# A hybrid decoder layer: the scaling of the exponentials, the sum of three attention branches and the order of their units are changed

## The chip, the cores and the metric

The kernel runs on one core of a Trainium2 chip as a single launch. The metric is the device time of one execution in microseconds; the median of several runs is given. A profile is one further execution, recorded by the hardware profiler. PE is the matrix engine (PEld its weight loads), DVE the vector engine, ACT the scalar engine, POOL the GpSimd engine, and SP the queue that issues most DMAs. Each engine works through its own instructions in order.

## The reference

One layer for 2048 tokens of width 1024, in float32:

```
h = RMSNorm(x); P = h @ W_in             # columns for three head groups
A: sliding-window attention (window 128, 4 heads, sinks, QK-norm, relative bias)
B: S5 state-space model, GELU, GLU
C: block attention, 4 heads, one key/value head, per block of 128 queries:
   o_cmp = softmax(q k_cmp + bias) v_cmp          # keys compressed 32 -> 1, stride 16
   top 16 of 32 key blocks by the compressed probabilities
   o_sel = softmax(q k_sel + bias) v_sel          # the selected blocks
   o_win = softmax(q k_win + bias) v_win          # the last 512 keys
   o     = gate0 * o_cmp + gate1 * o_sel + gate2 * o_win
x = x + W_out @ concat(RMSNorm(o_A), RMSNorm(o_B), RMSNorm(o_C))
x = x + W_down @ relu(W_up @ RMSNorm(x))^2
```

The compressed keys and values come from a two-layer network over 32 tokens: a hidden layer of 128 with GELU, then 64 outputs.

## The kernel before

The program runs in stages. The front (`phase_front`) computes the projection; in its second half the products of each chunk are merged with the steps of the state-space model (`ssm_steps`). Then a middle stage runs three lists of steps merged evenly with one another: sliding-window attention (`swa_steps`), the GLU (`glu_steps`) and a list with the bias tables and the compression of keys and values (`bias_steps`, `compress_steps`). Then comes block attention with the output projection (`phase_mix`), then the up projection and the down projection, both as seven-product schemes over halves.

Where exactness is wanted, a float32 operand is split into a rounded high part and a low part (fp32r), and a product is the sum of two or three products of parts (`mm3`, lines 76 to 78).

Block attention goes over 16 blocks of 128 queries. For each block the kernel loads and normalises queries and keys (`prep`), computes the compressed branch (`cmp_steps`), from block 8 on selects key blocks (`select`), and then runs four *units*: two pairs of heads of the window branch (up to 640 keys), and two pairs of the selected branch (all keys so far, up to 2048, with a mask in the lower rows of the query operand). A unit has two lists of steps:

- `logits` (lines 860 to 884): for up to 512 keys at a time, two products into one of two PSUM banks (`pq`, lines 875 and 876), one DVE pass that adds the bias, writes the negated logits to a slab in SBUF and keeps the running minimum (line 878), and after the last piece one ACT exponential over the whole slab with its sum (line 883).
- `pv` (lines 886 to 906): for two blocks of 128 keys and two heads, four PE transposes of the exponentials into one PSUM bank (`pp`, line 896, two banks), an ACT copy to the high part (line 899), a DVE subtraction to the low part (line 900), and the value products from both parts (line 904) into a PSUM sum (`po`). These products are given a lower priority (`LAG`).

At the end of each of the three branches, `combine` (lines 908 to 924) copies the sum from PSUM (ACT, line 913), turns it back by four transposes (line 917), multiplies it by gate over sum of exponentials (DVE, line 919), and POOL adds the two parts, high and low of the values, to the block's output (lines 921 and 924).

The order of the work: lists of steps are merged evenly (`merge`). In the loop over blocks, the value products of unit u are merged with the logits of unit u+1, with the steps of the next block that come ahead of its units (`front`: `prep`, the compressed branch, `select`), and with a share of a queue of *finish* steps of older blocks (`finish_steps`: load, scaling, the turn of the mixed row, 48 products with the output weights, the residual sum, the square for the norm). The finish products are fillers: they have a lowered priority. The framework's scheduler takes this order and the priorities, and fixes each engine's order of instructions and the semaphores. For the last block the selected units come first and the window units last.

Buffers of block attention: four slabs of 2048 floats for the exponentials of both branches, PSUM with two banks for logits, two for transposed exponentials, two for sums, one for turns (`pt`) and one for the filler (`pw`). From block 2 on (`open_late`) the output weights are loaded and the norms of the other two head groups are prepared, by steps on DVE (lines 44 to 54).

## Time and profile before

| what | value |
|---|---|
| median of 3 runs | 2577.39 us (2571.8 to 2578.93) |
| the profiled execution | 2574.28 us, its span 2572.5 us |
| busy share of the span | PE 96%, PEld 81%, DVE 69%, ACT 52%, POOL 44% |
| mean granted PE clock | 0.987 |
| front with state-space model | about 0 to 416 us |
| sliding-window attention, GLU, compression | about 416 to 616 us |
| block attention, with the rest of the GLU and the output projection | about 616 to 1277 us |
| up projection | about 1277 to 1955 us |
| down projection | about 1955 to 2572 us |

How to read it: the busy time of an engine counts every instruction from start to end. A product's record is longer than the time until the next one can start, since products are pipelined, so a busy PE is not a PE at its pace. A line in the groups gives the line of the kernel, engine, operation, what is written and read, shape and count; then busy time and mean duration of one; then the idle time of the engine in front of them with what ended it. The chain of waits is the work that ended last, followed back from the end; a piece's time there is counted from the end of the piece before.

### The profile page before, as it was taken

How to read it: one execution, taken by the hardware profiler on the slowest of the kernel's cores; microseconds unless marked ns; L12 is line 12 of the kernel's file. 1: busy time of each engine (PE TensorE's matmuls, PEld its weight loads, DVE VectorE, ACT ScalarE, POOL GpSimd, SP SyncE). 2: the span in 40 equal slices, each digit the busy share in tenths (PEclk: the TensorE clock that was granted, in tenths of full speed). 3: DMA queues.
4: the chain of work that ended last, by engine and by line, in shares of the span. 5: the costliest groups of instructions: out<-in, count | busy, mean ns of one | idle time of the engine just before them, and what ended most of it. 6: DMA issues, size and time to landing. Idle time of an engine off the chain costs nothing.

```text
span 2572.5 us, 38493 instructions
## 1 busy us (share of the span) xinstructions
PE 2475.1 (96%) x12904; PEld 2080.1 (81%) x12904; DVE 1769.6 (69%) x3455; ACT 1324.9 (52%) x2767; POOL 1119.3 (44%) x1168
## 2 busy tenths in 40 slices
PE   8999998999999999999999999899999999999999
PEld 8989997777787777777777888688887888888887
DVE  4744876864787677777465565765557888888886
ACT  5334546765676565655465554544444444344442
POOL 3045222222223233332476767565545344454447
PEclk9999999999989999999999999999999999999999
DMA  6153426221212121221566667755547534444435
GB/s 199 61 126 102 116 89 172 86 60 50 65 64 71 36 67 48 87 66 56 177 204 187 187 185 207 233 163 144 153 130 251 167 93 136 132 132 130 123 98 197
DMA packets 397144, 324.66 MB, mean 126 GB/s; under 512 B 51943, under 2 KB 363885, under 8 KB 395121
## 3 DMA queue, kind: packets, MB, share of 16 engines
q1 hardware_dynamic: 360848, 297.03, 38.6%
q10 hardware_dynamic: 36096, 25.17, 3.1%
q8 instruction: 102, 1.67, 0.3%
q14 instruction: 98, 0.79, 0.1%
HBM read 209.66 MB, written 112.45 MB: 125 GB/s over the span
## 4 chain that ended last, share of the span: by engine, by line
PE 67%; DVE 5%; issue 2%; ACT 2%; DMA 2%; POOL 1%; SPq 0%; DVEq 0%; POOLq 0%; ACTq 0%
PE pdc L1738 7%; PE pdb L1738 7%; PE pda L1738 7%; PE pub L1556 6%; PE puc L1556 6%; PE pua L1556 6%; PE pdd L1738 3%; PE pud L1556 3%; PE pw L76 2%; PE pps L896 2%; PE pos L904 2%; PE pw L77 2%; PE pw L78 2%; DVE sls L878 1%; PE gpm L76 1%
## 5 line engine op out<-in xcount | busy, mean ns | idle before, releaser
L1414 ACT CAST v<-vr 128x512 fp32r<-128x512 f32 x224 | 139.4, 624 | 304.2 <-DMA vr<-vd 148.4
L1415 DVE TENSOR_TENSOR v<-vr,v 128x512 fp32r<-128x512 f32 x224 | 233.1, 1048 | 81.2 <-ACT v L1414 79.2
L1738 PE MATMUL pdc<-dw,v 128*128 128x512 f32 x768 | 187.0, 392 | 4.3 <-ACT dw L1414 3.2
L1738 PE MATMUL pdb<-dw,v 128*128 128x512 f32 x768 | 185.2, 390 | 0.0
L1738 PE MATMUL pda<-dw,v 128*128 128x512 f32 x768 | 184.5, 389 | 0.0
L1527 POOL TENSOR_TENSOR fs<-ur,ur 128x512 f32<-128x512 f32 x64 | 94.8, 1481 | 189.2 <-DMA ur<-in_w_up 152.0
L1738 PEld LDWEIGHTS pdc<-dw,v 128*128 128x128 f32 x768 | 145.3, 189 | 35.4 <-ACT dw L1414 3.7
L1738 PEld LDWEIGHTS pdb<-dw,v 128*128 128x128 f32 x768 | 144.8, 189 | 30.3
L1738 PEld LDWEIGHTS pda<-dw,v 128*128 128x128 f32 x768 | 144.1, 188 | 30.0
L1414 ACT CAST uh<-fs 128x512 fp32r<-128x512 f32 x128 | 78.5, 621 | 152.0 <-PE pub L1556 62.7
L1415 DVE TENSOR_TENSOR ul<-fs,uh 128x512 fp32r<-128x512 f32 x128 | 134.3, 1051 | 22.6 <-ACT uh L1414 22.3
L1415 DVE TENSOR_TENSOR ul<-ur,uh 128x512 fp32r<-128x512 f32 x96 | 101.0, 1053 | 52.3 <-ACT uh L1414 48.5
L900 DVE TENSOR_TENSOR tls<-pps,ths 128x512 fp32r<-128x512 f32 (+1 forms) x144 | 93.2, 658 | 46.0 <-ACT ths L899 37.7
L899 ACT CAST ths<-pps 128x512 fp32r<-128x512 f32 (+1 forms) x144 | 79.5, 565 | 83.4 <-PE pos L904 40.3
L76 PE MATMUL pw<-wo_h,mh 128*128 128x512 f32 x256 | 109.2, 427 | 6.2 <-ACT mh L1251 4.2
L1572 POOL TENSOR_TENSOR ev<-e,e 128x512 f32<-128x512 f32 x64 | 95.9, 1498 | 31.9 <-ACT e L1569 21.9
L1556 PE MATMUL pua<-fh,ul 128*128 128x512 f32 x256 | 100.9, 394 | 5.7 <-DVE ul L1415 5.7
L78 PE MATMUL pw<-wo_h,ml 128*128 128x512 f32 x256 | 105.4, 412 | 0.0
L77 PE MATMUL pw<-wo_l,mh 128*128 128x512 f32 x256 | 105.1, 410 | 0.0
L1556 PE MATMUL puc<-fh,uh 128*128 128x512 f32 x256 | 102.1, 399 | 1.9 <-DVE eu L1565 1.9
L1556 PE MATMUL pub<-fh,uh 128*128 128x512 f32 x256 | 102.1, 399 | 1.6 <-ACT fh L1414 1.6
L1556 PE MATMUL pua<-fh,uh 128*128 128x512 f32 x256 | 101.0, 395 | 2.5 <-ACT e L1576 2.5
(573 smaller groups left out, 7875.3 us busy)
## 6 DMA issues: line engine op xcount, KB each, us to landing
vr<-vd SPq DMA_DIRECT2D x224, 256.0 KB
ur<-in_w_up SPq DMA_DIRECT2D x128, 256.0 KB
vd<-ev SPq DMA_DIRECT2D x128, 256.0 KB
vd<-e ACTq DMA_DIRECT2D x64, 256.0 KB
dr<-in_w_down SPq DMA_DIRECT2D x32, 512.0 KB
x<-in_x SPq DMA_DIRECT2D x16, 512.0 KB
mx<-in_x SPq DMA_DIRECT2D x16, 512.0 KB
x<-mx ACTq DMA_DIRECT2D x16, 512.0 KB
```

Of the source, the lines that this page charges most:

```text
L76: nc.tensor.matmul(out, sh, mh, start=first, stop=False)
L77: nc.tensor.matmul(out, sh, ml, start=False, stop=False)
L78: nc.tensor.matmul(out, sl, mh, start=False, stop=last)
L896: nc.tensor.transpose(pt[:, j, hh], sls[hh][:, (b0 + j) * P:(b0 + j + 1) * P], C["ident"])
L899: nc.scalar.copy(th[:, 0:nb], pt[:, 0:nb])
L900: nc.vector.tensor_tensor(tl[:, 0:nb], pt[:, 0:nb], th[:, 0:nb], op=ALU.subtract)
L1414: nc.scalar.copy(dh, src)
L1415: nc.vector.tensor_tensor(dl, src, dh, op=ALU.subtract)
L1527: nc.gpsimd.tensor_tensor(t, x, y, op=op)
L1556: nc.tensor.matmul(bank[b], w[:, k], h[o][:, k], start=first and k == 0 and n == 0, stop=k == HALF - 1 and n == 2, skip_group_check=True)
L1572: nc.gpsimd.tensor_tensor(tile_("v" + o), x, y, op=op)
L1738: nc.tensor.matmul(bank[b, q], x[:, q, j], y[:, j], start=first and j == 0 and n == 0, stop=j == 1 and n == 2, skip_group_check=True)
```

## The change

In block attention:

- Window and selected branch: after the exponential, DVE takes the reciprocal of each head's sum, and POOL multiplies the whole slab by it and by the gate. The compressed branch is scaled likewise after its reciprocals (`recip`). `combine` is called once for each block, without weights; a DVE reduction adds high and low parts.
- All three branches add into one PSUM sum of the block (`po` moves to `front`); only its first product starts the bank, and the other products of that kind are issued behind it. The bank is released by the copy in `combine`. There is one such bank in place of two; the transposed exponentials have three in place of two.
- The value products of a unit are merged with the logits of the unit two places on. The value products of the compressed branch lie with those of the block's first unit. The window branch has four slabs of its own of 640 floats.
- The turn of an older row (`next_turned`) is placed behind the fifth filler product; the output step writes its squares to SBUF and not to PSUM; the norms in `open_late` are computed by POOL.

In the front and in the middle stage:

- The last four half products of the front come behind the last steps of the state-space model.
- The compression's activations are stored so that a product of the hidden layer reads neighbouring elements; before, it read every eighth one.
- Six empty steps are appended to the list with bias tables and compression, so that its steps come earlier in the merge.

The core of the diff:

```diff
-        run(merge(rest, ssm_steps(tc, C, S, u_st, dkp, dca, tp, ps_g, ps_t)))
+        run(merge(rest[:-4], ssm_steps(tc, C, S, u_st, dkp, dca, tp, ps_g, ps_t)) + rest[-4:])
...
-        X = box["X"] = tp.tile([P, 1040], F32, tag="X", name=f"cX{st}")
-        nc.sync.dma_start(X[:, 1024:1040], cmp_pos[0, st].rearrange("(jj two) d -> (two d) jj", two=2))
+        X = box["X"] = tp.tile([P, 8, 130], F32, tag="X", name=f"cX{st}")
+        for b in range(2):
+            nc.sync.dma_start(X[:, :, 128 + b], cmp_pos[0, st, 16 * b:16 * b + 16].rearrange("(jj two) d -> (two d) jj", two=2))
...
-        nc.scalar.copy(box["X"][:, 512 * q:512 * q + 512], pt.rearrange("p a b -> p (a b)"))
+        nc.scalar.copy(box["X"][:, :, 64 * q:64 * q + 64], pt.rearrange("p a (m j) -> p j (a m)", j=8))
...
-            nc.tensor.matmul(ph, w1[:, jj], X[:, jj:jj + 8 * P + 1:8], start=jj == 0, stop=jj == 15)
+            nc.tensor.matmul(ph, w1[:, jj], X[:, jj % 8, jj // 8:jj // 8 + P + 1], start=jj == 0, stop=jj == 15)
...
                 nc.scalar.activation(x, x, AF.Exp, bias=nm[:, h:h + 1], scale=-1.0, accum_out=den[:, h:h + 1])
+                if gate is not None:
+                    nc.vector.reciprocal(den[:, h:h + 1], den[:, h:h + 1])
+                    nc.gpsimd.tensor_scalar(x, x, den[:, h:h + 1], gate, op0=ALU.mult, op1=ALU.mult)
...
-            pt = self.ps_p.tile([P, 2, 2, P], F32, tag="pp", name=f"pp{name}{b0}", bufs=2)
+            pt = self.ps_p.tile([P, 2, 2, P], F32, tag="pp", name=f"pp{name}{b0}", bufs=3 if self.lag else 2)
...
-                        nc.tensor.matmul(po, v_of(b0 + j), t[:, j].rearrange("p h q -> p (h q)"),
-                                         start=b0 + j == 0 and n == 0, stop=b0 + j == nblk - 1 and n == 1)
+                        opening = b0 + j == 0 and n == 0 and first is not None
+                        begun = first.get("mm") if opening else None
+                        with self.tc.issue_after(begun) if begun is not None else nullcontext():
+                            mm = nc.tensor.matmul(po, v_of(b0 + j), t[:, j].rearrange("p h q -> p (h q)"), start=opening and begun is None,
+                                                  stop=last and b0 + j == nblk - 1 and n == 1, skip_group_check=True)
+                        if opening and begun is None:
+                            first["mm"] = mm.ins
...
+        if w is None:
+            nc.vector.tensor_reduce(acc, pt.rearrange("p h a d -> p h d a"), axis=AX.X, op=ALU.add)
+            return
...
-            rsqrt_into(nc, sm, ra, ss_a, 1.0 / 256, NT, "ra")
-            rsqrt_into(nc, sm, rc, ss_b, 0.25 / 512, NT, "ra")
+            rsqrt_into(nc, sm, ra, ss_a, 1.0 / 256, NT, "ra", nc.gpsimd)
+            rsqrt_into(nc, sm, rc, ss_b, 0.25 / 512, NT, "ra", nc.gpsimd)
...
+                if i >= 8:
+                    pn = box["pn"] = lp.tile([P, 4, P], F32, tag="qd", name=f"pn{i}", bufs=1)
+                    nc.gpsimd.tensor_tensor(pn[:, :, 0:n], slc[:, :, 0:n], den.unsqueeze(2).broadcast_to([P, 4, n]), op=ALU.mult)
+                nc.gpsimd.tensor_tensor(slc[:, :, 0:n], slc[:, :, 0:n], w.unsqueeze(2).broadcast_to([P, 4, n]), op=ALU.mult)
...
-                    box[h] = lp.tile([P, L], F32, tag="sl", name=f"sl{nm_}{i}{h}", bufs=4)
+                    width, tag = (5 * P, "slw") if nm_ == "w" else (L, "sl")
+                    box[h] = lp.tile([P, width], F32, tag=tag, name=f"sl{nm_}{i}{h}", bufs=4)
...
-                nc.scalar.activation(pw, xt, AF.Square, accum_out=box["ss"][:, n:n + 1])
+                nc.scalar.activation(late["fp"].tile([P, 512], F32, tag="sq", name=f"xsq{i}{n}"), xt, AF.Square, accum_out=box["ss"][:, n:n + 1])
...
+            before = late.pop("turn", [])
+            res[8:8] = before
...
-            res[1:1] = late.pop("turn", [])
...
+            res = units(i, *box["q"], box["oc"], box["po_of"])
+            res[0] = (res[0][0], box["cmp"][1] + res[0][1])
...
-            for u in range(3):
-                acc += cuts[u]
-                na, nt = len(ahead) * acc // tot, len(tail) * acc // (tot + len(cur[3][1]))
-                for st in merge(cur[u][1], cur[u + 1][0], ahead[done_a:na], tail[done_t:nt]):
-                    st()
+            for u in range(4):
+                if u == 2 and i + 1 < NT:
+                    ocs[i + 1] = box["oc"]
+                    nxt = units_of(i + 1, box)
+                acc = sum(size[:u + 1])
+                na, nt = len(ahead) if i + 2 == NT and u else max(min(1, len(ahead)), len(ahead) * acc // tot), len(tail) * acc // tot
+                new = cur[u + 2][0] if u < 2 else nxt[u - 2][0] if nxt else []
+                run(merge(cur[u][1], new, ahead[done_a:na], tail[done_t:nt]))
...
-            run(merge(swa, glu[:cut], b_nsa + c_steps))
+            run(merge(swa, glu[:cut], b_nsa + c_steps + [lambda: None] * 6))
```

More of the change, by code (lines that the diff above doesn't have):

```diff
@@ L857, in late, with logits @@
         return self.tc.high_priority(offset=-n) if n else nullcontext()
-    def logits(self, sl_of, h, qA, qB, chunks, m0, nm, den, name):
+    def logits(self, sl_of, h, qA, qB, chunks, m0, nm, den, name, gate=None):
         nc = self.nc
@@ L917, in combine @@
                 nc.tensor.transpose(pt[:, h].rearrange("p a d -> p (a d)"), oT[:, h * P:(h + 1) * P], self.C["ident"])
+        if w is None:
+            nc.vector.tensor_reduce(acc, pt.rearrange("p h a d -> p h d a"), axis=AX.X, op=ALU.add)
+            return
         t = lp.tile([P, 4, 2, 64], F32, tag="ot", name=f"ot{name}", bufs=1)
         nc.vector.tensor_tensor(t, pt, w.unsqueeze(2).unsqueeze(3).broadcast_to([P, 4, 2, 64]), op=ALU.mult)
-        if first:
-            eng.tensor_tensor(acc, t[:, :, 0], t[:, :, 1], op=ALU.add)
-        else:
-            for a in range(2):
-                eng.tensor_tensor(acc, acc, t[:, :, a], op=ALU.add)
+        eng.tensor_tensor(acc, t[:, :, 0], t[:, :, 1], op=ALU.add)
     def normed(self, dst, o, name, eng=None):
@@ L1187, in units @@
                     for h in (2 * pair, 2 * pair + 1):
-                        ls += A.logits(lambda h=h, box=box, nm_=nm_: slab(h, box, nm_), h, qA, qB, chunks_of(h), -NEG, nm, den, f"{nm_}{i}")
-                    ps = A.pv(lambda pair=pair, po=po: po()[:, 256 * pair:256 * pair + 256], lambda pair=pair, box=box: [box[2 * pair], box[2 * pair + 1]],
-                              v_of, nblk, f"{nm_}{i}{pair}")
-                    if pair == 1:
-                        ps.append(close)
+                        ls += A.logits(lambda h=h, box=box, nm_=nm_: slab(h, box, nm_), h, qA, qB, chunks_of(h), -NEG, nm, den, f"{nm_}{i}", gt[:, h, b:b + 1])
+                    ps = A.pv(lambda pair=pair: po()[:, 256 * pair:256 * pair + 256], lambda pair=pair, box=box: [box[2 * pair], box[2 * pair + 1]],
+                              v_of, nblk, f"{nm_}{i}{pair}", None, end)
+                    if end and pair == 1:
+                        ps.append(lambda: A.combine(po(), None, oc, f"c{i}"))
                     res.append((ls, ps))
@@ L1311, in finish_steps @@
                 over = [lambda k=k: filler(0, k) for k in range(3, 6)] + [lambda k=k: filler(1, k) for k in range(6)]
-                end = [lambda: A.normed(box["mix"][:, 768:D], oc, f"c{i}", nc.vector), lambda: turned(6, 8, ps_p, "pp", 2)]
+                end = [lambda: A.normed(box["mix"][:, 768:D], oc, f"c{i}", nc.vector), lambda: turned(6, 8, ps_p, "pp", 3)]
                 return early, over, end + [lambda n=n, k=k: filler(n, k) for n in range(2) for k in (6, 7)]
@@ L1315, in finish_steps @@
             res = [load, lambda: turned(0, 4), lambda: turned(4, 8)] + [lambda n=n, k=k: filler(n, k) for n, k in order]
+            before = late.pop("turn", [])
+            res[8:8] = before
             if i >= NT // 2:
-                res.insert(8, blocks)
-                res.insert(13, block_sums)
-            res[1:1] = late.pop("turn", [])
+                res.insert(8 + len(before) * 3, blocks)
+                res.insert(13 + len(before) * 3, block_sums)
             if i < NT // 2:
@@ L1329, in front, with po @@
             box = {}
+            def po():
+                if "po" not in box:
+                    box["po"] = ps_o.tile([P, 512], F32, tag="po", name=f"poc{i}")
+                return box["po"]
+            box["po_of"] = po
             def start():
@@ L1333, in start @@
                 box["oc"] = lp.tile([P, 4, 64], F32, tag="oc", name=f"oc{i}", bufs=6)
-                box["cmp"] = cmp_steps(i, *box["q"], box["oc"])
-            n = 4 + 1 + 2 + 1 + (i >= 8)
-            return box, [start] + [lambda k=k: box["cmp"][k]() for k in range(n)]
+                box["cmp"] = cmp_steps(i, *box["q"], po)
+            n = 4 + 1 + (i >= 8)
+            return box, [start] + [lambda k=k: box["cmp"][0][k]() for k in range(n)]
         def units_of(i, box):
-            return units(i, *box["q"], box["oc"])
+            res = units(i, *box["q"], box["oc"], box["po_of"])
+            res[0] = (res[0][0], box["cmp"][1] + res[0][1])
+            return res
         box, steps = front(0)
```

60 lines of the change are left out of this document (21 added, 39 removed).

## The prediction

> **What bounds the kernel now.** I read the head of the page first, then the busy time by stretch, then the chain of waits, and last the groups of each engine in the attention stage.
>
> ```profile
> span 2572.5 us, 38493 instructions
> PE 2475.1 (96%) x12904; PEld 2080.1 (81%) x12904; DVE 1769.6 (69%) x3455; ACT 1324.9 (52%) x2767; POOL 1119.3 (44%) x1168
> ```
> ```profile
> 580.00:616.00 36.00, 32.16 (x152) 25.52 (x151) 8.71 (x26) 9.96 (x30) 6.40 (x10) 1.00 0.19 55
> 625.00:1277.00 652.00, 616.88 (x3744) 509.63 (x3744) 471.23 (x1374) 398.84 (x967) 214.40 (x447) 0.98 0.22 69
> 700.00:720.00 20.00, 16.28 (x63) 13.26 (x63) 17.22 (x41) 12.69 (x25) 5.88 (x12) 0.52 0.53 175
> 720.00:1240.00 520.00, 493.85 (x3046) 407.23 (x3046) 379.90 (x1099) 316.88 (x743) 167.43 (x360) 0.99 0.20 61
> ```
>
> The columns are the stretch, its length, then busy time and count of PE, PEld, DVE, ACT and POOL, the granted clock, the DMA share and the rate. The change touches the stretches from 410 to 1277 us: sliding-window attention (SWA) to about 580, the end of the compression to 616, block attention after that. PE is busy for 95% of block attention, DVE for 72%, ACT 61%, POOL 33%: PE is the engine to shorten. But 95% is not 95% of its pace. The groups tell how much is left:
>
> ```profile
> L76 PE MATMUL pw<-wo_h,mh 128*128 128x512 f32 x235 | 99.0, 421 | 1.9 <-DVE ml L1252 1.4 <-ACT pw L1267 0.3
> L875 PE MATMUL pqs<-kAs,qA 128*128 128x512 f32 x112 | 49.8, 444 | 5.7 <-DVE mx L878 4.4 <-DVE nms L878 0.6 <-DVE nmc L878 0.3
> L896 PE MATMUL pps<-c_ident,sls 128*128 128x128 f32 x544 | 93.1, 278 | 4.5 <-DVE tls L900 2.0 <-ACT sls L883 1.4 <-DVE rat L52 0.3
> L896 PE MATMUL ppw<-c_ident,slw 128*128 128x128 f32 x276 | 55.8, 292 | 1.7 <-DVE nmc L878 0.7 <-ACT slw L883 0.5 <-DVE tls L900 0.2
> L904 PE MATMUL pos<-ths,Vs 128*128 128x256 f32 x272 | 68.7, 307 | 1.1 <-ACT ths L899 0.9
> L904 PE MATMUL pow<-thw,vw 128*128 128x256 f32 x138 | 38.0, 328 | 1.2 <-ACT thw L899 1.1
> ```
> ```profile
> 1012.64 0.44 PE ptow L917 x4
> 1018.42 0.23 PE pw L77
> 1022.13 0.24 PE pos L904 x2
> ```
>
> The second fence is the chain, which gives a piece's own time where neighbours overlap: 0.23 us for a product of 512 columns, 0.12 for one of 256, 0.11 for a transpose. Lines 76 to 78 issue 705 such products and lines 875 and 876 another 224 for the selected keys, 929 x 0.23 = 214 us; the value products are 2 x (272 + 138) x 0.12 = 98 us; the transposes 820 x 0.11 = 90 us; the remaining 1175 or so, mostly small, at 0.11, are 129 us. That is 531 of 652 us, so about 120 us (an estimate) are late starts, of which the busy time shows 35 as idle. This is the pot for a better order; the other pot is PE work that goes away.
>
> **The change, part by part.** Everything is set against the profiled execution, 2574.3 us, with a span of 2572.5; the median of the runs, 2577.4, is 3 us above it.
>
> *Compression, hidden layer.* The activations are laid out so that a product reads 129 neighbouring elements instead of every eighth.
>
> ```profile
> 521.35 7.64 PE cph L765 x32
> 588.12 7.74 PE cph L765 x32
> ```
> ```profile
> 407.32 1.05 PE L570 MATMUL pv<-U,BT 128*128 128x128 f32 x8
> 408.13 0.42 PE L76 MATMUL pm_c<-wh_c,hh 128*128 128x396 f32 x1
> 408.39 0.34 PE L77 MATMUL pm_c<-wl_c,hh 128*128 128x396 f32 x1
> 408.57 0.34 PE L78 MATMUL pm_c<-wh_c,hl 128*128 128x396 f32 x1
> ```
>
> Both pieces are wholly on the chain: 64 at 0.24 us. The nearest contiguous fp32 products, eight of 128 columns, start within 407.32 to 408.13, 0.10 us each. 64 x 0.14 gives -9 us; the bounds are 0 (the stride costs nothing and the fp32 weights do) and -9. I take -9, because the two groups differ in the stride and one column only. The copy that now reads PSUM with a stride and one more short DMA per stream lie beside PE.
>
> *SWA's ends.* The last four half products of the front are moved behind the scan's end: 4 x 12 products at 0.18 us (408.39 to 408.57), 8.6 us of PE work that can lie over the start of SWA, where PE waits for POOL:
>
> ```profile
> 419.94 0.55 PE L825 MATMUL ptqa<-c_ident,qda 128*128 128x128 f32 x3 [0.89 <-POOL qda L818]
> ```
>
> Bounds 0 and -8.6; I take -4, as the stalls are short and the scan loses that much cover. The six empty steps pull bias and compression forward into the first 15/21 of SWA, so that the second hidden product and its ACT and DVE chain no longer stand alone behind 580 us. PE idles for 3.8 us there (32.16 of 36): bounds 0 and twice that, as the busy time hides late starts, taken -3.
>
> *One sum in place of three.* Exponentials are multiplied by gate over sum before they are transposed, so compressed, window and selected values add up in one bank, and one turn back remains of three for each of the 16 query blocks.
>
> ```profile
> L917 PE MATMUL ptos<-c_ident,oTs 128*128 128x128 f32 x64 | 11.2, 291 | 2.0 <-ACT oTs L913 1.9
> L919 DVE TENSOR_TENSOR ots<-ptos,ws 128x512 f32<-128x512 f32 x16 | 11.0, 687 | 6.1 <-PE ptos L917 6.1
> L1182 DVE RECIPROCAL dens<-dens 128x4 f32<-128x4 f32 x16 | 2.8, 173 | 0.9 <-ACT sls L883 0.8
> L1141 DVE TENSOR_REDUCE pm<-pn 128x128 f32<-128x512 f32 x1 | 1.1, 1094 | 0.0
> L913 ACT COPY oTs<-pos 128x512 f32<-128x512 f32 x16 | 9.4, 585 | 3.7 <-PE pos L904 3.6
> ```
>
> PE: 32 groups of four transposes at 0.44 us go, -14 us. ACT: 32 copies x 0.585 = -19 us. DVE: 48 multiplies x 0.687 = -33 and 32 reciprocals x 0.173 = -6, against 128 single reciprocals at about 0.17 (+22) and 16 reductions at about 1.1 (+18): even. Neither ACT nor DVE is full, so only PE's -14 is counted; bounds 0 (PE would have waited anyway) and -16, with the 2.0 us of idle time in front.
>
> POOL gets the scaling:
>
> ```profile
> L1239 POOL TENSOR_SCALAR mix<-mix,r_b 128x512 f32<-128x512 f32 x16 | 11.2, 700 | 5.8 <-DVE dens L1182 5.8
> L1276 POOL TENSOR_SCALAR mx<-mx,rr 128x1024 f32<-128x1024 f32 x8 | 8.9, 1118 | 0.8
> L48 POOL TENSOR_SCALAR nqt<-nr,nqh 128x1 f32<-128x1 f32 x45 | 16.1, 357 | 4.3
> L44 POOL TENSOR_SCALAR nqh<-ns 128x1 f32<-128x1 f32 x15 | 3.0, 197 | 48.9 <-ACT mix L931 48.5
> L924 POOL TENSOR_TENSOR oc<-oc,ots 128x256 f32<-128x256 f32 x32 | 23.5, 735 | 79.9 <-DVE ots L919 77.0 <-DVE denw L1182 1.7
> ```
>
> 512 more elements cost 418 ns, 0.82 each, with 0.28 us fixed, and a second scalar from memory 0.16 (357 against 197). A window slab of 640 is 0.96 us, a full slab of 2048 2.1 us. The 128 slabs hold 128 x 4 x (70 + 136) = 105,472 elements: 86 + 128 x 0.44 = 143 us, with the compressed slabs and the moved norm steps some 160. Five additions a block go, 80 x 0.735 = 59 us. POOL rises from 214 to about 315 of 650 us, 49%: enough in sum, hidden so long as it is not late.
>
> *Value products two units behind, third bank, window slabs of their own.* A unit is two heads of one branch; 652 us hold 64 of them, 10 us each, so exponentials and scaling get a lead of about 20 us where they had 10 or less. What this can free is what PE's loads wait for:
>
> ```profile
> PEld pqs L875 <- DVE mx L878: 10.0, 18, 1.4
> PEld pps L896 <- DVE tls L900: 7.8, 22, 2.1
> PEld pps L896 <- ACT sls L883: 4.8, 12, 1.2
> ```
>
> The first is the logits' own pair of banks and stays. The second is the pair of turn banks that becomes three, the third the exponentials: 12.6 us named, with window and compressed alike perhaps twice that, and part of the unseen late starts. Bounds +5 and -40 (a third of the 120); I take -12, near the named rows.
>
> *What it costs.* One bank for the sum: the first value product of a block must wait for the last one's copy, 0.585 us and ACT's queue, 15 times: 0 to +30 if ACT is 2 us behind (a full exponential); filler products lie over most, +5. In the last block the selected slabs are still held by the block before, as there are four; there the lead is one unit, as before: 0. The square in the output step no longer holds the filler's bank: 32 x 0.6 us at most, taken -3.
>
> *The slow stretch.* At 700 to 720 us the clock is 0.52 and 63 matmuls pass where 60 us before had 347 (116 in 20 us):
>
> ```profile
> 640.00:700.00 60.00, 57.49 (x347) 47.66 (x345) 44.17 (x156) 41.96 (x124) 16.63 (x28) 1.00 0.19 56
> 699.43 0.66 PE L917 MATMUL ptoc<-c_ident,oTc 128*128 128x128 f32 x4 [1.21 <-ACT oTc L913]
> 701.94 1.11 PE L896 MATMUL pps<-c_ident,sls 128*128 128x128 f32 x4 [1.85 <-DVE tls L900]
> ```
>
> 20 x (1 - 63/116) = 9 us are lost. DVE carries two norm chains here (lines 44 to 54), which the change gives to POOL, and the turn transposes in front go for two branches of three. Bounds 0 and -9; taken -6. The Trainium skill, "TensorE: Matmul & The Clock Gate" (What's actually happening), has the clock halve after an idle window of about 3.4 us; here pauses of 1.2 and 1.85 us close together came before it, so the row shows it more easily tripped than the rule; by the rule alone the term would be the full -9, by the row it may trip again elsewhere.
>
> The sum: -9 - 4 - 3 - 14 - 12 + 5 - 3 - 6 = -46, to a profiled time of 2528 and a median of about 2531 us.
>
> **The rivals.** *Only the removed work counts* (-9, -14, +5): the order gains nothing, as DVE's and ACT's steps between transposes and value products set the pace as before. 2559 us. For it: DVE is at 73% between 720 and 1240 us and each pair of key blocks still needs one ACT and one DVE pass. Against: the waits of those passes are what the third bank lengthens.
>
> *Slower: POOL's queue.* POOL works in order, and it now stands between exponential and transpose:
>
> ```profile
> POOL xq L1271 <- ACT pw L1267: 93.0, 14, 18.7
> ```
>
> If scalings are queued behind this step, which waits for a finished output row, they are late by its wait: 6.6 us in the mean, 18.7 at most, below the lead of about 20. It decides once the wait and a few scalings of 2.1 us exceed the lead. Then PE loses up to the 93 us: 2577 - 46 + 93 = 2624.
>
> *Selection late.* The selected logits of a block now follow its selection at once, where two units lay between. Operations of DVE with two inputs in SBUF stretch while POOL is at work:
>
> ```profile
> L1132 DVE TENSOR_TENSOR wc<-denc,gt x16: 152/164/858, 617.3 to 1169.4; 128x4 f32<-128x4 f32 x16
> ```
>
> Minimum, median and maximum: 0.16 us becomes 0.86, about one POOL operation. With POOL operations of 2 us and three such steps in each selection, 8 selections lose up to 6 us each; half of it, +24, makes 2555. The Trainium skill's "GPSIMD Engine Reference" (Key points) names such contention with VectorE instructions that have two SBUF inputs, and the row agrees.
>
> *Nothing moves*: the removed waits are replaced by others: 2574. *More*: the lead frees the full 40 us: 2503.
>
> **How the numbers follow.** Forecast 0.50, only the work 0.17, selection late 0.08, more 0.07, nothing 0.08, POOL's queue 0.10. 0.3% (8 us) is about what measurement can tell from no change. Faster is the first four less their tails, 0.80; same 0.09; slower 0.11. The range goes from 2498 (most of the -40 and -9) to 2578 (nothing moves); the slow case and a little of the far gain are left out.
>
> **What would show it.** Right: the hidden product takes 3 to 4 us in place of 7.7; four transposes a block in the turn; no clock of 0.5 near the loading of the output weights; block attention about 35 us shorter with POOL near half busy; transposes that no longer wait for exponentials. Wrong: transposes waiting for POOL's scaling, first value products waiting for the sum's copy, selected logits waiting for the selection, or the same stage length with fewer PE instructions.

## The result, and the profile after

The changed kernel takes 2550.3 us (median; 2547.6 to 2554.3), the kernel before, timed beside it, 2576.4 us: a ratio of 0.9903, 95% interval 0.9890 to 0.9915. The gain is 26 us where 46 were forecast. The time lies inside the range, 19 us above the forecast and 9 us below the rival "only the removed work counts". All ratios below are to the kernel before on the same chip, with 95% intervals; one thousandth is 2.6 us. The profiled execution took 2547.6 us, the lowest of the four.

The head of the page after:

```profile
span 2545.8 us, 38321 instructions
PE 2436.4 (96%) x12776; PEld 2058.3 (81%) x12776; DVE 1761.2 (69%) x3456; ACT 1307.9 (51%) x2735; POOL 1205.9 (47%) x1263
```

PE has 128 rows fewer, the 128 transposes of the two turns that went. The hidden layer of the compression, by the timeline of PE, after (start, duration, line, columns, count):

```profile
499.33 3.84 PE L766 MATMUL cph<-cX,cw 128*128 128x129 f32 x32
557.55 3.84 PE L766 MATMUL cph<-cX,cw 128*128 128x129 f32 x32
```

7.7 us became 3.8, twice. Busy time by stretch, first of the kernel before (columns as in the prediction: the stretch, its length, PE, PEld, DVE, ACT and POOL with counts, granted clock, DMA share, rate). The first row reaches from block attention's first logits to the first product of the feed-forward's upper half, the last row over the 115 us behind that:

```profile
612.90:1303.50 690.60, 649.87 (x3890) 535.12 (x3890) 495.95 (x1443) 419.41 (x1019) 234.81 (x467) 0.97 0.24 75
1303.50:1418.50 115.00, 110.57 (x481) 88.58 (x480) 67.56 (x75) 63.73 (x112) 74.88 (x55) 0.99 0.66 195
```

and of the changed kernel:

```profile
594.30:1282.40 688.10, 633.27 (x3822) 533.14 (x3823) 486.62 (x1453) 408.20 (x998) 329.62 (x565) 0.97 0.25 77
680.00:700.00 20.00, 14.02 (x83) 12.17 (x83) 10.03 (x38) 11.34 (x32) 12.52 (x43) 0.83 0.38 100
700.00:720.00 20.00, 14.05 (x60) 11.11 (x60) 13.24 (x29) 11.68 (x23) 8.26 (x15) 0.74 0.43 139
1282.40:1397.40 115.00, 115.00 (x516) 93.66 (x515) 74.32 (x78) 67.32 (x123) 72.48 (x55) 1.00 0.67 198
```

Block attention begins 18.6 us earlier (612.9 to 594.3), ends 21.1 us earlier, and is only 2.5 us shorter. The remaining 5.5 us lie behind it, where the diff changes nothing. In the 115 us after the boundary PE now works through 516 instructions where it worked through 481, at a clock of 1.00 and 0.99: it waits less. But the same 5440 PE instructions behind the boundary take between 1262.8 and 1270.4 us in the traces of this document, so it is not shown that the change earns these 5.5 us. POOL is busy for 48%, as forecast. PE's busy time fell by 17 us and the stage did not.

The first row hides two things. Not all of the 18.6 us is gain: part of it is work handed on. The gated linear unit's products in this stage, before and after (first and last start, then count):

```profile
L77 PE MATMUL gpm<-glu_l,zh x40: 387/393/483, 612.7 to 687.6; 128*128 128x512 f32 x40
```
```profile
L77 PE MATMUL gpm<-glu_l,zh x55: 387/393/486, 595.1 to 680.3; 128*128 128x512 f32 x55
```

Counted from the stage's first logits, 52 such products of 512 columns and 8 transposes more lie in it: 52 x 0.227 + 8 x 0.11 = 12.7 us. They cancel the 14 us of turns that went, so the stage's work is the same (571 and 570 us, at one fixed price per shape, such as 0.227 us for 512 columns and 0.11 for a transpose) and so are its late starts (119.5 and 118.3 us). But these late starts have changed their nature. Sorting every PE instruction of the stage by how much later than its predecessor's price it starts gives, worked out from the traces (us, with counts; "under 0.1" is net of instructions that start early):

```
                     under 0.1   0.1 to 1.5    over 1.5     sum
before                  20.4     93.4 (379)    5.7 (2)    119.5
after                   17.6     66.6 (295)   34.2 (12)   118.3
after, no scaling       18.9     67.7 (282)   19.2 (5)    105.6
 same, lead of one      18.3     67.1 (283)   13.8 (3)     99.3
after, lead of one      20.1     88.6 (357)   38.7 (11)   147.4
after, two turn banks   19.6     78.0 (310)   25.7 (9)    123.4
all norms on DVE        18.7     77.4 (327)   20.4 (9)    116.4
after, lead of three    21.7     81.4 (331)   44.8 (11)   147.8
```

By size, some 27 us of short stalls went, and ten long ones of 28 us came. The sorting says nothing of causes: after a long stall the next operands may already be there, so that a long stall takes in short ones. In the three versions listed that scale and have a lead of two, the sum stays at 116 to 123 us while the long stalls lie anywhere from 20 to 34 and the short ones from 67 to 78.

The waits of PE in the stage, first of the kernel before (engine, tile and line, what it waited for: us in total, times, longest). Of the names, sls, slw and slc are the slabs of the selected, window and compressed branch, pps, ppw and ppc their transposes, tls and tlw the low parts of these, poc the one sum; ptx is the turn of a mixed row, mh and ml its two parts, pw the filler's bank, mx a finished output row and pth its turn:

```profile
PE pqs L875 <- DVE mx L878: 5.6, 12, 1.0
PE pw L76 <- ACT mh L1251: 4.2, 2, 3.6
PE pps L896 <- DVE tls L900: 2.0, 2, 1.9
```

and of the changed kernel:

```profile
PE pth L1283 <- DVE mx L1263: 6.8, 5, 1.8
PE pps L900 <- POOL sls L887: 5.4, 1, 5.4
PE ppc L900 <- POOL slc L1140: 4.5, 1, 4.5
PE poc L911 <- DVE tls L904: 4.4, 2, 4.2
PE pw L76 <- ACT mh L1250: 4.4, 2, 3.7
```

Single waits of 4 to 5 us, where the kernel before had none above 2 us except at its end. The wait of 5.4 us (5.7 from one start to the next) is seen on PE's and POOL's timelines:

```profile
688.68 0.28 PE L877 MATMUL pqw<-kBw,qB 96*128 96x128 f32 x1
694.35 0.47 PE L900 MATMUL pps<-c_ident,sls 128*128 128x128 f32 x1 [5.40 <-POOL sls L887]
```
```profile
686.88 0.19 POOL L44 TENSOR_SCALAR nqh<-ns 128x1 f32<-128x1 f32 x1
...
691.70 0.40 POOL L52 TENSOR_TENSOR rat<-rat,rah 128x16 f32<-128x16 f32 x2
692.08 0.47 POOL L941 TENSOR_SCALAR mix<-oc,nr 128x256 f32<-128x256 f32 x1
...
693.34 0.20 POOL L1072 TENSOR_SCALAR r_c<-r_c 128x16 f32<-128x16 f32 x1
693.53 0.77 POOL L887 TENSOR_SCALAR sls<-sls,dens,gt 128x512 f32<-128x512 f32 x1
```

The slab needs 0.77 us of POOL and gets it 6 us late (DVE had its reciprocal at 687.5), behind two norm chains and the norm of a mixed row. The fourth row of the list (poc behind tls) is mostly one wait that ends at 1059.2 us: tls stands on DVE behind the selection's reduction, and that waits for POOL:

```profile
1057.61 0.93 DVE L1147 TENSOR_REDUCE pm<-pn 128x112 f32<-128x448 f32 x1 [4.10 <-POOL pn L1139]
```

So the reading after the result was: POOL's queue takes back what the new order wins. The groups of POOL's scalings, after, for their price:

```profile
L887 POOL TENSOR_SCALAR sls<-sls,dens,gt 128x128 f32<-128x128 f32 (+15 forms) x64 | 81.2, 1268 | 107.3 <-DVE dens L886 87.6 <-PE ppw L900 7.4 <-PE pw L78 4.6
L887 POOL TENSOR_SCALAR slw<-slw,denw,gt 128x640 f32<-128x640 f32 (+4 forms) x64 | 52.9, 827 | 119.1 <-DVE denw L886 96.0 <-PE ptx L1248 8.5 <-PE pqs L877 4.5
```

134 us for 128 scalings, where 143 had been worked out; POOL mostly stands idle before them, waiting for the reciprocal (87.6 and 96.0 us). Over the stage it is far from full; what would count, by this reading, is what stands ahead of a slab in its queue at a few places. The experiments test this.

### The profile page after: what moved, and what is told of

Its sections match the earlier page's. It is cut to its first block, busy times and chain, and to the rows that moved or that the text cites. A ratio compares the mean times of both kernels' runs of the same rounds, so it can differ in the third digit from the quotient of the medians.

```text
span 2545.8 us, 38321 instructions
## 1 busy us (share of the span) xinstructions
PE 2436.4 (96%) x12776; PEld 2058.3 (81%) x12776; DVE 1761.2 (69%) x3456; ACT 1307.9 (51%) x2735; POOL 1205.9 (47%) x1263
## 4 chain that ended last, share of the span: by engine, by line
PE 63%; DVE 6%; POOL 3%; DMA 3%; issue 3%; ACT 2%; SPq 0%; ACTq 0%; DVEq 0%; POOLq 0%
PE pdc L1744 7%; PE pdb L1744 7%; PE pda L1744 7%; PE pub L1562 6%; PE puc L1562 6%; PE pua L1562 6%; PE pdd L1744 3%; PE pud L1562 3%; PE poc L911 3%; PE pw L76 2%; PE pps L900 2%; PE pw L77 2%; PE pw L78 2%; PE pqs L876 1%; PE pqs L877 1%
## 5 line engine op out<-in xcount | busy, mean ns | idle before, releaser
L887 POOL TENSOR_SCALAR sls<-sls,dens,gt 128x128 f32<-128x128 f32 (+15 forms) x64 | 81.2, 1268 | 107.3 <-DVE dens L886 87.6
L900 PE MATMUL pps<-c_ident,sls 128*128 128x128 f32 x544 | 102.3, 281 | 8.2 <-POOL sls L887 5.4
L887 POOL TENSOR_SCALAR slw<-slw,denw,gt 128x640 f32<-128x640 f32 (+4 forms) x64 | 52.9, 827 | 119.1 <-DVE denw L886 96.0
```

What stands on the lines that cost most here:

```text
L887: nc.gpsimd.tensor_scalar(x, x, den[:, h:h + 1], gate, op0=ALU.mult, op1=ALU.mult)
L900: nc.tensor.transpose(pt[:, j, hh], sls[hh][:, (b0 + j) * P:(b0 + j + 1) * P], C["ident"])
```

## The experiments

**Norm chains of open_late back on DVE.** The direct test of the 5.7 us wait.

```
-            rsqrt_into(nc, sm, ra, ss_a, 1.0 / 256, NT, "ra", nc.gpsimd)
+            rsqrt_into(nc, sm, ra, ss_a, 1.0 / 256, NT, "ra")        # and the same for rc
```

> The changed kernel with one part undone: the two norm chains of open_late (lines 44 to 54 on 16 columns, and the halving of r_c) are DVE's again. In the profile of the changed kernel PE stands still for 5.7 us at 688.7 us and 4.9 us at 708.6 us, waiting for slabs whose scaling is queued on POOL behind these steps and behind the norm of a mixed row. Theory A (POOL's queue made the long stalls there): both stalls shrink to under 1.5 us, the granted clock of 680 to 720 us (0.83 and 0.74) rises, and the time falls by 8 to 12 us, to about 2540. Rival B (only the removed products count; PE lost 20 us in the same 60 us of the kernel before, 26 now): the stall goes back to DVE's chain, 2546 to 2552, at most 4 us better.

Ratio 0.9903 (0.9887 to 0.9918), the changed kernel's. The two waits of 5.7 and 4.9 us became two of 3.2 and 3.3 (and one of 1.6), the clock in 680 to 720 us is 0.85 and 0.81, and the stage is 0.8 us shorter. Rival B. The first of the two is still a slab's, behind the norm of a mixed row on POOL; the second is for DVE, which now has the chains. So the run moves the chains, it does not take them away.

**Turn of the previous row ahead again.** The diff also moves the transposes of the previous block's output row between the halves of the output step, which the prediction had left out.

```
-            res[8:8] = before
+            res[1:1] = before          # after the two inserts, which stand at 8 and 13 again
```

> The changed kernel with one part undone that my prediction did not price: the turn of the previous block's output row (pth) stands again ahead of a block's output step, not between its two halves. In the changed kernel PE waits at these transposes for DVE's addition at line 1263, which frees the one bank of the output step: 6.8 us in 5 waits, beside 6.5 us on the loads. Theory A (the new place costs what these waits say): 5 to 8 us faster than the changed kernel, about 2544. Rival B (the waits move to the scaled row, as pth waited for POOL 4.2 us before the change): within 2 us, 2548 to 2552.

Ratio 0.9912 (0.9899 to 0.9926): no difference from the changed kernel that can be told. Rival B; the waits moved: 5.4 us of the output step's products behind DVE's addition and 4.1 us of pth behind POOL.

**No scaling.** The multiplications by gate over sum are left out, so the rows come out unweighted.

```
-                    nc.gpsimd.tensor_scalar(x, x, den[:, h:h + 1], gate, op0=ALU.mult, op1=ALU.mult)
-                nc.gpsimd.tensor_tensor(slc[:, :, 0:n], slc[:, :, 0:n], w.unsqueeze(2)...)
```

> The changed kernel without the multiplications of the exponentials by gate over sum (the 128 slabs and the 16 compressed ones), so the block attention's rows come out unweighted; the reciprocals stay. It prices POOL's place between exponential and transpose: its queue and its 150 us of work. Theory A (POOL's queue is behind three of the four longest stalls in block attention, 5.7, 4.9 and 4.5 us, and DVE's operations with two SBUF inputs stretch less): 14 to 22 us faster than the changed kernel, 2528 to 2536. Rival B (the lead of two units hides the scaling but for a few us): 0 to 5 us faster, 2545 to 2550.

Ratio 0.9848 (0.9835 to 0.9861), 2533 us: 14 us below the changed kernel, at the edge of A's numbers. This is the price of the scaling as a whole. The long stalls fall from 34 to 19 us, the short ones stay (67 and 68). The stage, and the waits of PE in it, without scaling:

```profile
589.60:1264.90 675.30, 633.05 (x3821) 532.68 (x3822) 479.30 (x1453) 405.37 (x998) 183.63 (x421) 0.97 0.24 79
PE pw L76 <- ACT mh L1248: 6.7, 2, 6.0
PE ptr L1076 <- DMA r_t<-r_d: 5.0, 1, 5.0
PE pps L899 <- DVE tls L903: 4.5, 2, 3.9
```

No slab is waited for any more. At the place of the 5.7 us wait PE now waits 5.0 us for the round trip of the norm factors, which go through memory before ptr; this wait may have lain hidden under that for the slab. It did not decide the run with the norm chains on DVE, where PE does not stand still at ptr.

The 14 us are not POOL's place in the path alone. DVE, with the same 1453 instructions in the stage, is busy for 479.3 us without the scaling and for 486.6 with it; the section on the hardware shows one of its operations stretched beside a scaling. How the 14 us divide between late slabs and slower DVE operations, no run separates.

**The strided hidden layer.**

```
-            nc.tensor.matmul(ph, w1[:, jj], X[:, jj % 8, jj // 8:jj // 8 + P + 1], ...)
+            nc.tensor.matmul(ph, w1[:, jj], X[:, jj:jj + 8 * P + 1:8], ...)      # with the old layout of X
```

> The changed kernel with the old layout of the compressed activations: 64 products read every eighth element again. The products took 0.233 us with the stride and 0.111 without, one after the other. Theory A (PE sets the end there, so PE time removed is time won): 7 to 9 us slower than the changed kernel, 2558. Rival B (in the new order the hidden layer lies beside sliding-window attention, which waits for other engines anyway): within 3 us, 2547 to 2553.

Ratio 0.9936 (0.9923 to 0.9948): 8.5 us slower than the changed kernel. Theory A; the layout is worth all of its PE time, as far as intervals of this width (some 5 us for the difference of two runs) can tell.

**Block attention's part alone.** The old ends of sliding-window attention (SWA) and the old hidden layer, the rest as changed.

```
-        run(merge(rest[:-4], ssm_steps(...)) + rest[-4:])
+        run(merge(rest, ssm_steps(...)))
-            run(merge(swa, glu[:cut], b_nsa + c_steps + [lambda: None] * 6))
+            run(merge(swa, glu[:cut], b_nsa + c_steps))                          # and the strided hidden layer
```

> The changed kernel with everything ahead of block attention undone: the scan takes all half products beside it again, no empty steps, the strided hidden layer. What stays is the block attention's part (one sum, scaled exponentials, lead of two units, third bank) with the turn's new place and the norms on POOL. The products' own work that falls away is 14 us there and 8 us ahead. Theory A (only the removed PE work counts, and the ends of sliding-window attention give nothing): about 14 us below the kernel before, ratio 0.9945, and 8 to 10 us above the changed kernel. Rival B (my prediction's sum, in which the ends and the hidden layer give 16 us and the block attention the rest): with 26 us measured in all, 10 us are left here, ratio 0.996. Rival C (the mix starts 18.6 us earlier in the changed kernel's trace and is only 2.5 us shorter, so that the gain lies ahead of it): ratio 0.998 or more.

Ratio 0.9934 (0.9922 to 0.9947), 17 us below the kernel before. Theory A's numbers; rival C, that the gain lies ahead of block attention, falls. (The trace shows less: the profiled execution took 2567.2 us, the slowest of five with a median of 2559.8.) And this kernel differs from the one with the strided hidden layer (0.9936) in the ends and the empty steps alone: these are worth 0, within about 5 us.

**Value products one unit behind.**

```
-            size = [len(cur[u][1]) + len(cur[(u + 2) % 4][0]) for u in range(4)]
+            size = [len(cur[u][1]) + len(cur[(u + 1) % 4][0]) for u in range(4)]
-                new = cur[u + 2][0] if u < 2 else nxt[u - 2][0] if nxt else []
+                new = cur[u + 1][0] if u < 3 else nxt[0][0] if nxt else []       # start and shares to match
```

> The changed kernel with the value products one unit behind the logits, as before the change, all else kept (one sum, scaling on POOL, three turn banks). A unit is some 10 us; the scaling by POOL comes between exponential and transpose. Theory A (the lead is what pays for POOL's place in the path): transposes wait for POOL's scaling, 10 us or more slower than the changed kernel, 2560 or more. Rival B (the lead moves nothing, as the waits are those of the turn banks and of DVE's and ACT's passes): within 4 us of the changed kernel, 2543 to 2551.

Ratio 0.9995 (0.9982 to 1.0007): 24 us slower than the changed kernel, the whole gain gone. The profiled execution took 2582.5 us, 10 us above the median of the twelve. Its waits of PE:

```profile
PE pps L900 <- POOL sls L887: 17.3, 18, 5.4
PE ppw L900 <- POOL slw L887: 12.9, 10, 3.6
PE pw L76 <- ACT mh L1250: 12.1, 1, 12.1
```

28 waits for scaled window and selected slabs, 30 us, where the list of two units has one, of 5.4. The third row is another matter. It lies in the last block, and 8 of the 29 us by which the stage is longer in this trace are there:

```profile
1296.07 2.44 ACT L1481 ACTIVATE fxr<-fxr,rr 128x1024 f32<-128x1024 f32 x2 [8.62 <-DMA fxr<-x]
```

ACT works in order, and ahead of the copy for which PE waits (mh, at 1307.3 us) stand instructions of the feed-forward, whose first waits for a load. Theory A for the rest.

**One unit behind, no scaling.** Both edits; the rows come out unweighted.

> The changed kernel with the value products one unit behind the logits and without the multiplications by gate over sum, so the rows come out unweighted. With the scaling the shorter lead cost 24 us (ratio 0.9995 against 0.9903); without the scaling, at the lead of two units, the ratio was 0.9848. Theory A (the longer lead mainly pays for POOL's place between exponential and transpose): without scaling the lead is worth little, ratio 0.985 to 0.989. Rival B (the lead is worth as much for ACT's and DVE's passes as for POOL): 18 us or more are lost, ratio 0.992 to 0.994.

Ratio 0.9845 (0.9830 to 0.9860), against 0.9848 with the lead of two. Theory A: without the scaling the longer lead is worth nothing, within about 5 us; with it, it is worth 24. The lead pays a debt that the scaling makes: 39 us at one unit, 14 at two.

**Two turn banks.**

```
-            pt = self.ps_p.tile([P, 2, 2, P], F32, tag="pp", ..., bufs=3 if self.lag else 2)
+            pt = self.ps_p.tile([P, 2, 2, P], F32, tag="pp", ..., bufs=2)        # and a pool of two
```

> The changed kernel with two turn banks in place of three; one PSUM bank stays unused. Before the change the loads of transposes waited 7.8 us for DVE's pass that frees the bank (DVE tls), and in the changed kernel the stalls of PE between 0.1 and 1.5 us have fallen from 93 to 67 us. Theory A (the third bank does that): 8 to 20 us slower than the changed kernel, 2555 to 2567. Rival B (the lead does it, or the planner's new order): within 4 us, 2543 to 2551.

Ratio 0.9901 (0.9888 to 0.9914): the third bank is worth nothing, within about 5 us, and rival B holds. The waits it was to end are there again (pps behind DVE tls, 7.3 us in 9, where the changed kernel has 2.4 in 3), and the short stalls are 11 us up; the long ones are 9 us down.

**All small norm chains on DVE.**

```
-        eng = eng or nc.gpsimd          # in normed; likewise open_late's two chains and the output rows'
+        eng = eng or nc.vector
```

> The changed kernel with all small norm chains of block attention on DVE in place of POOL: the two of open_late, that of each block's combined row (some 3.4 us on POOL for eight dependent steps of one column) and that of each finished output row. Without any scaling POOL's place in the path was worth 14 us. Theory A (the scalings are late because these chains stand before them in POOL's queue): 6 to 12 us faster than the changed kernel, about 2538; the stall of 4.5 us behind the selection goes. Rival B (it is the scalings' own work, 150 us, and what it does to DVE; or DVE, 72% busy and in order, now waits for ACT's squares in POOL's place): 2545 or slower.

Ratio 0.9897 (0.9884 to 0.9910): within 2 us of the changed kernel, rival B. POOL's part of the stage falls from 330 to 245 us, DVE's rises from 487 to 523. The long stalls fall from 34 to 20 us and the short ones rise from 67 to 77. POOL's queue was shorter and the sum the same. As DVE has the chains instead, 36 us more of work, this does not say that they cost nothing on POOL.

**Scaling in the transpose.** POOL scales the 128 columns of the identity, and the product with it turns and scales at once.

```
-                    nc.gpsimd.tensor_scalar(x, x, den[:, h:h + 1], gate, op0=ALU.mult, op1=ALU.mult)
+                    nc.gpsimd.tensor_scalar(dg, self.C["ident"], den[:, h:h + 1], gate, op0=ALU.mult, op1=ALU.mult)
-                    nc.tensor.transpose(pt[:, j, hh], blk, C["ident"])
+                    nc.tensor.matmul(pt[:, j, hh], blk, dgs_of()[hh], start=True, stop=True)
```

> The changed kernel with the scaling of window and selected slabs taken out of POOL's long operations: POOL multiplies the identity (128 columns) by gate over sum once a head, and the transposes become fp32 products of the slab with this diagonal, which turn and scale in one. The output is the reference's. POOL's 128 operations fall from 134 us (0.83 and 1.27 us each) to some 65 (an estimate: 0.28 + 128 x 0.82 ns + 0.16 each), and their latency to about 0.5 us; PE's products of 128 fp32 columns took 0.10 to 0.11 us beside 0.11 for a transpose. Theory A (the scalings' own length is what stands in the path): 6 to 12 us faster than the changed kernel, ratio 0.986 to 0.988. Rival B (it is their place behind other work in POOL's queue, or what a wait for a reciprocal holds up): ratio 0.989 to 0.991. Rival C (an fp32 product is dearer than a transpose where their weights change each time, 820 times): slower than the changed kernel.

Ratio 1.0135 (1.0116 to 1.0154): 60 us slower than the changed kernel, rival C. The first of the two groups of PE:

```profile
L905 PE MATMUL pps<-dgs,sls 128*128 128x128 f32 x1088 | 165.3, 278 | 4.8 <-POOL dgs L888 4.2 <-DVE tls L909 0.4
```

1088 rows where the transposes had 544 (and 556 for 276 in the window branch): an fp32 product is issued as two, each with its own weight load, and a transpose as one. That adds some 820 x 0.11 = 90 us of PE work; the stage is 57 us longer, so its late starts fell from 118 to 85. What the shorter scaling won, 33 us at most (a busier PE also hides waits), cost 90. The expectation took rows for products: in the hidden layer, too, 16 products a stream are 32 rows.

**The same with the norm chains on DVE.**

> The kernel with the diagonal, and with all small norm chains of block attention on DVE too, so that POOL's queue is short as well as its operations. Theory A (length and place both count): 2 to 6 us faster than with the diagonal alone. Rival B (with short scalings the queue no longer matters, and DVE's 290 more small operations cost as much): the same within 2 us, or slower.

Ratio 1.0114 (1.0097 to 1.0131), 5 us better than with the diagonal alone: A's size, though the two intervals overlap.

**A lead of three units.**

```
-                new = cur[u + 2][0] if u < 2 else nxt[u - 2][0] if nxt else []
+                new = cur[3][0] if u == 0 else nxt[u - 1][0]      # the next block's start in the first quarter
```

> The changed kernel with the value products three units behind the logits in place of two (two again at the last block); the steps of the next block's start, with its compressed logits and its selection, move into the first quarter of a block, behind the compressed value products. From one unit to two the lead won 24 of the 38 us that lie between the kernel with one unit and the one without scaling (ratios 0.9995, 0.9903, 0.9848). Theory A (what is left, 14 us, is late scalings too): the third unit wins 4 to 10 us more, ratio 0.986 to 0.989. Rival B (what is left lies where a lead doesn't reach: compressed slabs, the product for the selection, mixed rows and output rows in POOL's queue): ratio 0.989 to 0.992. Rival C (the start steps, all in one quarter, crowd DVE and ACT): 0.993 or more.

Ratio 0.9976 (0.9965 to 0.9987), 19 us slower than the changed kernel: rival C. Waits of PE:

```profile
PE ptx L1248 <- DVE mx L1263: 12.6, 1, 12.6
PE pw L76 <- DVE ml L1251: 11.9, 6, 5.0
PE ptr L1077 <- DMA r_t<-r_d: 6.9, 1, 6.9
```

POOL's slabs are gone from the list; in their place PE waits mostly for DVE. But the crowding of the start steps that C names is not shown to be the cause. The longest wait lies in the last block, where no next block starts:

```profile
1287.77 1.90 ACT L1428 CAST fh<-fl 128x2048 fp32r<-128x2048 f32 x1 [12.57 <-DMA fl<-sums]
1289.69 2.29 DVE L1429 TENSOR_TENSOR fl<-fl,fh 128x2048 fp32r<-128x2048 f32 x1 [14.10 <-ACT fh L1428]
```

DVE's addition, for which PE waits, stands behind an instruction of the feed-forward, that one behind ACT, and ACT waits for a load: the same trap as with the lead of one, and some 9 us dearer than the changed kernel's wait at that place (4.1). The profiled execution is 6 us above the median. So the run doesn't say what three units alone are worth. No version that computes the layer beats the changed kernel by more than can be measured.

## Why the prediction was half right

*Hidden layer, -9: right.* Undone, it costs 8.5 us, within about 5. The Trainium skill, "Advanced Engine Details and Errata" (SBUF Cachelines), has every access to another 16-byte line pay; here a 32-byte stride took 0.24 us a row and the neighbouring columns 0.12.

*SWA's ends, -4 and -3: wrong, 0.* The four half products do lie behind the scan (they end at 417 us) and not over SWA's stalls: SWA's first transposes start at 427.2 us, 7.3 us later (before at 419.9), and it takes as long as before (its last turn at 582.6, before 576.7 us). In the 10 us between, PE meets new waits, for the loads of the bias tables. The first of these loads is issued at 414.7 us, before at 407.3, just as much later as SWA; before, the half products beside the scan lay over it:

```profile
419.78 1.10 PE L712 MATMUL bpfs<-Ts,c_anti 128*128 128x512 f32 x2 [2.15 <-DMA Ts<-rs]
424.46 1.10 PE L712 MATMUL bpf<-T,c_anti 128*128 128x512 f32 x2 [1.56 <-DMA T<-r]
```

The six empty steps do bring the compression forward: its last product is at 564 us, before 603. But what leaves the tail is filled by the gated unit's products that would have covered something else, and 12.7 us of those move on into block attention. The step that failed is pricing the moved work by the idle time that it leaves, and not by the work that has to take its place.

*One sum in place of three, -14 on PE, DVE and ACT even and not counted: PE right by its rows, the rest perhaps too low.* With the ends at 0 the parts are: 26 us in all, 8.5 hidden layer, some 17 block attention. Without scaling block attention's part is 31 (39 - 8.5): the 14 us of transposes and another 17. In the traces most of these are late starts, 119.5 to 105.6 us: short stalls fall by 26, long ones rise by 13. The short ones fall as far without scaling and with the lead of one (67.1), so without the scaling the lead is not what makes them fall. What made them fall stays open. One candidate is the single sum, with two waits for a turn less in each block (ptos alone stood 2.0 us idle and held ACT and DVE in its chain) and fewer copies on ACT; another is the third bank (with two, the short stalls are 11 us up, though the sum only 5). No run undid the single sum alone.

The pot of late starts itself was a little large: at the prices of their real widths, the products of 625 to 1277 us leave some 105 us, not 120, since more than those counted have 512 columns.

*POOL's scaling, counted 0: the step that failed.* Its load was right (134 us against 143, POOL at 48%), and its cover was named, the lead of 20 us. It costs 14 us under that cover. The step read the share of busy time of an engine in order and set the mean lead against the single operation, 2 us. At the places shown, chains of small steps stood ahead of a slab, 6 us and more long, which the change itself partly put there. That these chains are what costs the 14 us is not shown: both runs that took them off POOL won nothing, and both gave them to DVE.

*Two-unit lead and third bank, -12: wrong as worked out, right that it was needed.* The bank is worth 0, within about 5 us. The lead is worth 24 us against the same kernel with one unit, and 0 without scaling; the named waits (DVE's and ACT's passes) were not what it pays for. Both terms together, lead and scaling, are what the prediction should have had as one: no gain at all, but a price of 14 us left over.

*Single bank, +5: too dear.* The list of waits after has no value product behind the sum's copy. *Square to SBUF, -3:* not isolated. *Slow stretch, -6: wrong.* The clock is 0.83 and 0.74 over 40 us where it was 0.52 over 20, and in 680 to 740 us the late starts are 26 us where they were 20. Giving the norm chains to POOL did not end it; with them on DVE again the clock is 0.85 and 0.81. The slow pieces, after:

```profile
692.00:698.80 6.80, 4.45 (x20) 4.15 (x20) 2.27 (x7) 3.82 (x8) 5.02 (x11) 0.50 0.43 137
702.20:705.60 3.40, 3.31 (x11) 2.38 (x12) 3.29 (x9) 3.33 (x7) 0.87 (x1) 0.50 0.51 162
712.40:719.20 6.80, 5.70 (x21) 5.12 (x22) 1.11 (x4) 3.21 (x7) 1.80 (x4) 0.50 0.24 80
```

The first and the third begin in the pauses of 5.4 and 4.5 us (idle time); ahead of the second the longest pauses are of 0.7 and 0.5 us. The rule that the prediction cites from the Trainium skill, "TensorE: Matmul & The Clock Gate" (What's actually happening), a halving after an idle window of about 3.4 us, fits the first and the third and not the second.

*The rivals.* "Only the removed work counts" came nearer in size (2559) and not in reason: more than the removed work was won, and the scaling took a part of it back. "Slower: POOL's queue" was right that slabs come late in POOL's queue, and wrong in place and price: step xq now waits 27.7 us in 9 where it waited 93 in 14, the late slabs shown stand behind norms and mixed rows, and the scaling costs 14 us of the 93 feared. "Selection late" did not come as described: in PE's list no selected logits wait for their selection, the operation of 0.86 us takes at most 0.38, and only the selection's product on POOL held DVE once, for 4.1 us. The turn's new place, which the prediction did not price, costs nothing that can be told.

## What to carry to other kernels

The busy share of an engine, here 48%, does not tell what it costs to put it between producer and consumer. Set the lead against the whole delay, with all that can stand ahead of an operation in the queue, and then measure the price by leaving the operation out. A longer lead is worth only what some latency in the path owes: price lead and latency as one term, and test each with and without the other, as the four kernels with one and two units, with and without scaling, do here. Taking waits away at one place changed the total by nothing that could be measured, three times: twice chains of steps went from one engine to another, once a turn changed its place. And look at the end of a stage: instructions of the next stage that wait for their loads can stand in an engine's queue ahead of the last block's.

## What the runs showed of the hardware

An fp32 product takes two rows of PE, each with a weight load and 0.11 us for 128 columns, and a transpose of the same fp32 block one; so turning and scaling by a diagonal costs some 90 us more of PE for 820 blocks. The Trainium skill, "FP8 and Floating Point Precision" (TensorE Precision Notes), gives true fp32 four passes; 0.22 us for 128 columns is 1.7 ns a column against 0.44 in the rounded (fp32r) products of 512 columns (0.227 us), four times as much, which agrees.

Eight dependent one-column steps of POOL hold its queue for 2.9 us (1045.45 to 1048.35) although their busy times add up to 2.2 (0.19, 0.19, then three times 0.34 and 0.26). Most start 0.36 to 0.45 us after the one before:

```profile
1046.83 0.34 POOL L48 TENSOR_SCALAR xrt<-rr,xrh 128x1 f32<-128x1 f32 x1
1047.27 0.26 POOL L49 TENSOR_SCALAR rr<-xrt,rr 128x1 f32<-128x1 f32 x1
1047.63 0.34 POOL L48 TENSOR_SCALAR xrt<-rr,xrh 128x1 f32<-128x1 f32 x1
```

At 693.5 us a slab found chains of this kind and a mixed row ahead of it.

A cast of DVE from SBUF to SBUF, with one input, took 0.22 us at the least and 1.50 us beside a scaling on POOL. It comes 16 times; the rows are before and after (minimum, median and maximum in ns), then the longest case after, with the scaling beside it. Without scaling its median is 0.24 us:

```profile
L1100 DVE CAST kBs<-kAs x16: 218/220/739, 615.1 to 1157.0; 64x128 fp32r<-64x128 f32 x16
L1108 DVE CAST kBs<-kAs x16: 219/408/1495, 596.8 to 1140.4; 64x128 fp32r<-64x128 f32 x16
1027.18 1.73 POOL L887 TENSOR_SCALAR sls<-sls,dens,gt 128x1664 f32<-128x1664 f32 x1 [6.01 <-DVE dens L886]
1027.50 1.50 DVE L1108 CAST kBs<-kAs 64x128 fp32r<-64x128 f32 x1
```

DVE's subtraction that reads PSUM (tls, 128x512) takes 0.69 us in the mean before, after and without scaling.
